# Hybrid encoder on one core: VectorE takes GpSimd's arithmetic in the mixers, and gates, branches and C keys are woven in a new order

## The chip, the core and the metric

The kernel runs on one core of a Trainium2 chip, with its engines TensorE (PE), VectorE (DVE), ScalarE (ACT), GpSimd (POOL) and SyncE (SP, which issues nearly all DMAs here). The metric is the device time of one execution in microseconds. Each engine runs its own list of instructions in order and waits on semaphores for the others.

## The reference

Two layers work on 272 tokens (256 on a grid of 4 rows by 64 columns, and 16 learned meta tokens) of width 1024, in float32:

```python
h = h + 0.5 * swiglu(rms_norm(h, ffn1_norm[l]), ffn1_w_in[l], ffn1_w_out[l])
h = h + hybrid_mixer(rms_norm(h, mix_norm[l]), ...)
h = h + 0.5 * swiglu(rms_norm(h, ffn2_norm[l]), ffn2_w_in[l], ffn2_w_out[l])
```

The mixer projects the normed tokens once into queries, keys and values for three attentions and into three gates, and sums the gated branches:

```python
qa, ka, va, qb, kb, vb, qc, kc, vc, gates = jnp.split(n @ w_in, offsets, axis=-1)
oa = window_sink_attention(rope(qa), rope(ka), va, sink)       # 8 query heads, 2 key heads, |i-j| <= 128
ob = neighbourhood_attention(qb, kb, vb, rpb)                  # 8 heads, 4 x 16 window, learned bias
oc = dense_block_attention(axial_rope(rms_norm(qc)), axial_rope(rms_norm(kc)), vc)
up = einsum('blnc,ncd->blnd', stack([oa, ob, oc]), w_branch)
return sum_n(sigmoid(gates) * up) @ w_out
```

Heads are 64 wide; d_ff is 2816. The last layer's outputs for meta tokens are not needed, so there 256 tokens are queried and 272 are keys.

## The kernel before

Activations lie transposed: features on the 128 partitions, tokens along the free dimension, so a matmul has 272 columns (256 where the meta tokens have dropped out). Float32 accuracy is made from two roundings: a weight block `raw` of 128x1024 is copied by ScalarE into a rounded `hi` (line 250) and the remainder `lo = raw - hi` is computed by VectorE (line 251). `mm` then issues three matmuls per block: hi by the rounded activations (L295), hi by their remainder (L296), lo by the rounded activations (L297). A projection to 256 features from 1024 (`plain(w, 0, 8, c0)`, two weight units of 128x1024) is 8 x 2 x 3 = 48 matmuls; a branch (`branch_rows`, one unit) is 24. The accumulators `acc` have two buffers, the score banks `s` three, weights `hi` and `lo` four each.

Inside the mixer every third plain unit's subtract goes to GpSimd (`lo_engine`), and units that are rearranged while they are split (`turned`, `pairs`: lines 236 to 248) give half of their subtracts to GpSimd. GpSimd also does one step of each rotary embedding (L787 for A, L835 for C) and one of the sums of gated branches (L909).

The mixer's order in the program is: the values, keys and queries of B (values and keys scaled by the row's norm at L762 and L766, queries at L773); then three attentions, each a generator that yields after the scores of one half of the heads for one block of 128 queries. Between two yields `weave` calls the next item of a list: during B the keys of A, the keys of C, both halves of A's queries; during A both halves of C's queries and then gates with branches of B; during C those of A; then those of C and `w_out`.

One step of an attention has the score matmuls (L518 for A and C, L684 for B) into banks `s`; VectorE's pass over each bank (L419 with mask, sink and minimum, or for C L424 and L425); ScalarE's exponential with its sum (L421, L426); VectorE's reciprocal (L438) and normalisation (L439, and L531 for the meta columns). One step later TensorE transposes the normalised `p` (L541; L696 in B), and after every second step multiplies by the values (L449, L454), and the result is split into `oh` and `ol` (L310, L311).

`gated(b, mp)` is a gate projection (48 matmuls), its scaling (L901), a tanh on ScalarE (L902), the branch (24 matmuls) and the product (L907). `c_keys` is a projection, its scaling (L842, L843), a square on ScalarE, matmuls that sum it over a head (L846), a reciprocal square root (`rsqrt`: square root on ScalarE, reciprocal L316 and one Newton step on VectorE), the rotary step and `stack_k` (L477, L479).

The order on each engine isn't that of the program alone: the framework's scheduler places instructions by their dependences and its own estimates of what they take, so matmuls of a woven projection stand between the scores and transposes of the attention. DMAs of weights go through SyncE's queue.

Of the kernel before, what the change touches and what calls it, by code (L numbers as in the profile page):

```python
# [17 lines left out]
D = 1024  # L18
# [74 lines left out]
def encoder_kernel(ctx: ExitStack, tc: tile.TileContext, x, meta_tokens, ffn1_norm, ffn1_w_in, ffn1_w_out,  # L93
# [57 lines left out]

    h = big.tile([128, 8, T], F32, name="h")
# [54 lines left out]
    sink = const.tile([128, DEPTH, 8], F32, name="sink")  # L207


    in_mixer = [False]  # L210
    unit_no = [0]

    def lo_engine():

        unit_no[0] += 1
        return POOL if in_mixer[0] and unit_no[0] % 3 == 0 else DVE

    def unit(nk, loads, pairs=False, turned=False):
# [9 lines left out]
        if turned:  # L228
# [3 lines left out]
            for g in range(2):  # L232
                for b in range(2):
# [3 lines left out]
                    (DVE if g else POOL).tensor_tensor(l_, r_, h_.bitcast(F32), op=ALU.subtract)  # L237
            if not pairs:
                hv, rv, lv = (t[:, :n].rearrange("p (k c) -> p k c", k=nk)[:, :, 128:] for t in (hi, raw, lo))
                ACT.copy(hv, rv)  # L240
                lo_engine().tensor_tensor(lv, rv, hv.bitcast(F32), op=ALU.subtract)
        elif pairs:
# [3 lines left out]
            for g in range(2):  # L246
                ACT.copy(hv[:, :, :, g], rv[:, :, g])
                (DVE if g else POOL).tensor_tensor(lv[:, :, :, g], rv[:, :, g], hv[:, :, :, g].bitcast(F32), op=ALU.subtract)
        else:
            ACT.copy(hi[:, :n], raw[:, :n])  # L250
            lo_engine().tensor_tensor(lo[:, :n], raw[:, :n], hi[:, :n].bitcast(F32), op=ALU.subtract)  # L251
# [61 lines left out]
    def rsqrt(dst, v, tmp):  # L313
# [5 lines left out]
        DVE.tensor_scalar(tmp, tmp, -0.5, 1.5, op0=ALU.mult, op1=ALU.add)  # L319
# [94 lines left out]
    def scores(p, i, s, den, mx, add, start, scale):  # L414
# [89 lines left out]
    def grouped(br, q, kk, vt, oh, ol, masks, mask_m, sinks, sink_m, rq, meta_queries):  # L504
# [3 lines left out]
        if rq is None:  # L508
            nsink = small()
            DVE.tensor_scalar(nsink, sinks, -1.0, None, op0=ALU.mult)  # L510

        def products(qi, half, pm):
            p, mx, den = wide(), small(), small()
            for i in range(4):
# [5 lines left out]
                if rq is None:  # L520
                    scores(p, i, s, den, mx, masks[qi], nsink[:, 4 * g + t:4 * g + t + 1], None)
# [37 lines left out]
        def meta_products():  # L559
# [3 lines left out]
            for g in range(2):  # L563
                for half in range(2):
                    DVE.tensor_copy(qm[:, g, g, half * 32:half * 32 + 32].rearrange("p (t j) -> p t j", t=2),
                                    q[half][:, g, :, GRID:])
# [8 lines left out]
            if rq is None:  # L575
                nsm = small()[:, :1]
                DVE.tensor_scalar(nsm, sink_m, -1.0, None, op0=ALU.mult)
# [455 lines left out]
```

## Time and profile before

| | us |
|---|---|
| median of 3 runs (1338.96 to 1340.93) | 1339.12 |
| the profiled execution | 1339.12 |
| its span | 1337.3 |
| TensorE busy, 10683 matmuls | 1308.9 |
| VectorE busy | 903.7 |
| ScalarE busy | 671.4 |
| GpSimd busy | 170.4 |

The granted clock of TensorE is 0.996 over the span. In rows of groups stand the line, engine, operation, output and inputs, shapes and count, then busy time and the mean of one in nanoseconds, then the engine's idle time before the group and what ended it. Rows in order of time begin with start and length in microseconds from the span's start. "PE busy" counts a matmul to its modelled end; in a steady stream the next one starts before that.

### The profile page before, as it was taken

The page shows a single profiled execution, that of the slowest core. Times are in us where ns is not written, and L with a number is a line of the kernel's source. Part 1 is how long each engine was busy: PE and PEld are TensorE (multiplying, and loading weights), DVE is VectorE, ACT ScalarE, POOL GpSimd, SP SyncE. Part 2 cuts the span into 40 slices and gives each one's busy share as a digit, 9 for nine tenths or more (in the row PEclk, how much of TensorE's full clock was granted, in tenths as well). Part 3 has the DMA queues.
Part 4 walks back from the last instruction along what each step waited for, and adds up shares of the span by engine and source line. Part 5 has one row for each costly group of instructions (what it writes and reads, how often), then busy time and mean ns, then how long its engine had stood idle before and what let it go on. Part 6 is the DMA issues. An engine that isn't in the chain of part 4 may idle for free. (4 is left out here: it accounts for less than half of the span.)

```text
span 1337.3 us, 26009 instructions
## 1 busy us (share of the span) xinstructions
PE 1308.9 (98%) x10683; PEld 1285.8 (96%) x10683; DVE 903.7 (68%) x1352; ACT 671.4 (50%) x1009; POOL 170.4 (13%) x115
## 2 busy tenths in 40 slices
PE   9999999988999999999999999999989999999997
PEld 8999999978999999999999999999889999999997
DVE  6655668699664587646676646677897567765663
ACT  6443444476554455434455434454776545543444
POOL 1000001332122220000000000022422233000000
PEclk9999999999999999999999999999999999999998
DMA  7765555532343676555565555555324456666652
GB/s 232 210 186 174 175 177 181 152 98 93 111 142 111 185 192 189 183 174 174 162 185 174 174 177 179 158 181 158 95 96 128 141 174 188 186 187 187 187 172 78
DMA packets 239010, 217.52 MB, mean 163 GB/s; under 512 B 24804, under 2 KB 237980, under 8 KB 238764
## 3 DMA queue, kind: packets, MB, share of 16 engines
q1 hardware_dynamic: 238540, 215.20, 53.1%
q8 instruction: 84, 1.38, 0.4%
q10 hardware_dynamic: 352, 0.66, 0.1%
q14 instruction: 34, 0.28, 0.1%
HBM read 214.78 MB, written 1.05 MB: 161 GB/s over the span
## 5 line engine op out<-in xcount | busy, mean ns | idle before, releaser
L250 ACT CAST hi<-raw 128x1024 fp32r<-128x1024 f32 (+1 forms) x386 | 398.6, 1033 | 551.6 <-PE acc L296 374.9
L296 PE MATMUL acc<-xl,hi 128*128 128x272 f32 (+1 forms) x2160 | 620.8, 287 | 0.0
L297 PE MATMUL acc<-xh,lo 128*128 128x272 f32 (+1 forms) x2160 | 619.2, 287 | 0.6 <-DVE lo L251 0.6
L295 PE MATMUL acc<-xh,hi 128*128 128x272 f32 (+1 forms) x2160 | 618.2, 286 | 0.6 <-DVE qk L766 0.6
L251 DVE TENSOR_TENSOR lo<-raw,hi 128x1024 fp32r<-128x1024 f32 (+1 forms) x349 | 424.1, 1216 | 215.3 <-ACT hi L250 213.0
L295 PEld LDWEIGHTS acc<-xh,hi 128*128 128x128 f32 x2160 | 408.1, 189 | 3.1 <-issue 2.7
L297 PEld LDWEIGHTS acc<-xh,lo 128*128 128x128 f32 x2160 | 406.8, 188 | 1.5 <-DVE lo L251 0.8
L296 PEld LDWEIGHTS acc<-xl,hi 128*128 128x128 f32 x2160 | 406.5, 188 | 1.1 <-issue 0.7
L296 PE MATMUL acc<-hl,hi 128*128 128x272 f32 (+1 forms) x704 | 201.9, 287 | 0.0
L297 PE MATMUL acc<-hh,lo 128*128 128x272 f32 (+1 forms) x704 | 201.1, 286 | 0.0
L295 PE MATMUL acc<-hh,hi 128*128 128x272 f32 (+1 forms) x704 | 200.4, 285 | 0.0
L295 PEld LDWEIGHTS acc<-hh,hi 128*128 128x128 f32 x704 | 132.7, 189 | 0.1
L297 PEld LDWEIGHTS acc<-hh,lo 128*128 128x128 f32 x704 | 132.3, 188 | 0.0
L296 PEld LDWEIGHTS acc<-hl,hi 128*128 128x128 f32 x704 | 132.2, 188 | 0.0
L251 POOL TENSOR_TENSOR lo<-raw,hi 128x1024 fp32r<-128x1024 f32 x37 | 91.6, 2475 | 229.2 <-ACT hi L250 217.4
L349 POOL TENSOR_TENSOR ss<-ss,scr 128x544 f32<-128x544 f32 (+1 forms) x12 | 17.4, 1448 | 602.2 <-ACT scr L346 602.1
L295 PE MATMUL acc<-oh,hi 128*128 128x272 f32 (+1 forms) x192 | 54.7, 285 | 0.0
L296 PE MATMUL acc<-ol,hi 128*128 128x272 f32 (+1 forms) x192 | 54.7, 285 | 0.0
L297 PE MATMUL acc<-oh,lo 128*128 128x272 f32 (+1 forms) x192 | 54.5, 284 | 0.0
L401 DVE TENSOR_TENSOR scr<-acc,scr 128x544 f32<-128x544 f32 (+1 forms) x40 | 28.6, 716 | 31.0 <-PE acc L297 30.9
L304 DVE SCALAR_TENSOR_TENSOR h<-acc,h 128x544 f32<-128x544 f32 (+1 forms) x40 | 28.5, 714 | 28.4 <-PE acc L297 28.3
L398 DVE TENSOR_TENSOR scr<-acc,rstd 128x544 f32<-128x544 f32 (+1 forms) x40 | 28.6, 716 | 26.2 <-PE acc L297 26.2
(257 smaller groups left out, 1367.1 us busy)
## 6 DMA issues: line engine op xcount, KB each, us to landing
raw<-in_ffn_w_in_dram SPq DMA_DIRECT2D x176, 512.0 KB, 3.6
raw<-in_ffn_w_out_dram SPq DMA_DIRECT2D x80, 512.0 KB, 3.4
raw<-in_w_in_dram SPq DMA_DIRECT2D x80, 512.0 KB, 3.8
raw<-in_w_in_dram SPq DMA_DIRECT2D x32, 256.0 KB, 3.2
raw<-in_w_branch_dram SPq DMA_DIRECT2D x32, 256.0 KB, 4.0
raw<-in_w_out_dram SPq DMA_DIRECT2D x16, 512.0 KB, 3.8
raw<-in_ffn_w_out_dram SPq DMA_DIRECT2D x16, 256.0 KB, 2.7
raw<-in_w_branch_dram SPq DMA_DIRECT2D x8, 512.0 KB, 3.4
```

The lines of the kernel that those rows point to most:

```text
L250: ACT.copy(hi[:, :n], raw[:, :n])
L251: lo_engine().tensor_tensor(lo[:, :n], raw[:, :n], hi[:, :n].bitcast(F32), op=ALU.subtract)
L295: PE.matmul(o, a, rh, start=k == 0, stop=False)
L296: PE.matmul(o, a, rl, start=False, stop=False)
L297: PE.matmul(o, b, rh, start=False, stop=k == len(rows) - 1)
L304: DVE.scalar_tensor_tensor(hv, a[:, :, :n], 0.5, hv, op0=ALU.mult, op1=ALU.add)
L349: (DVE if j == 3 else POOL).tensor_tensor(ss, ss, dst, op=ALU.add)
L398: DVE.tensor_tensor(g, gate, rb, op=ALU.mult)
L401: DVE.tensor_tensor(g, up, g, op=ALU.mult)
```

## The change

- Inside the mixers VectorE does all of GpSimd's arithmetic: the subtracts of `unit`, the rotary steps and the addition of branch A. GpSimd keeps memsets and, outside the attentions, the sums of squares of a norm (L349).
- The keys of C are computed among B's projections, between B's keys and B's queries.
- A gate and its branch are two functions, and three plans say which pieces follow which yield: in B the keys of A, a half of A's queries, a gate, the other half, another gate; in A branches of B, C's queries and two gates; in C the pairs of branch A and two gates of branch C.
- Small operations: copies of meta columns go from VectorE to ScalarE; the sinks are reordered and negated once; a few scalings by a constant (`tensor_scalar`) become operations that read the constant from a tile `cc`; the factor 0.125 of C's queries is folded into the constant under the root.

```diff
@@ -148,6 +148,10 @@
     POOL.memset(ones, 1.0)
+
+    cc = const.tile([128, 4], F32, name="cc")
+    for i, v in enumerate((1.5, HD * EPS, -1.0)):
+        POOL.memset(cc[:, i:i + 1], v)
...
-    def lo_engine():
-
-        unit_no[0] += 1
-        return POOL if in_mixer[0] and unit_no[0] % 3 == 0 else DVE
+    sinks_tg = const.tile([128, 2, DEPTH * 8], F32, name="sinks_tg")
...
-                    (DVE if g else POOL).tensor_tensor(l_, r_, h_.bitcast(F32), op=ALU.subtract)
+                    DVE.tensor_tensor(l_, r_, h_.bitcast(F32), op=ALU.subtract)
...
-                (DVE if g else POOL).tensor_tensor(lv[:, :, :, g], rv[:, :, g], hv[:, :, :, g].bitcast(F32), op=ALU.subtract)
+                DVE.tensor_tensor(lv[:, :, :, g], rv[:, :, g], hv[:, :, :, g].bitcast(F32), op=ALU.subtract)
...
             ACT.copy(hi[:, :n], raw[:, :n])
-            lo_engine().tensor_tensor(lo[:, :n], raw[:, :n], hi[:, :n].bitcast(F32), op=ALU.subtract)
+            DVE.tensor_tensor(lo[:, :n], raw[:, :n], hi[:, :n].bitcast(F32), op=ALU.subtract)
...
-        DVE.tensor_scalar(tmp, tmp, -0.5, 1.5, op0=ALU.mult, op1=ALU.add)
+        DVE.scalar_tensor_tensor(tmp, tmp, -0.5, cc[:, :1].to_broadcast(list(tmp.shape)), op0=ALU.mult, op1=ALU.add)
...
-            DVE.tensor_scalar(mx[:, i:i + 1], mx[:, i:i + 1], scale, -1.0, op0=ALU.mult, op1=ALU.mult)
+            DVE.scalar_tensor_tensor(mx[:, i:i + 1], mx[:, i:i + 1], scale, cc[:, 2:3], op0=ALU.mult, op1=ALU.mult)
...
-        DVE.tensor_copy(vrep, vt[:, None, GRID:].to_broadcast([128, 8, META]))
+        ACT.copy(vrep, vt[:, None, GRID:].to_broadcast([128, 8, META]))
...
-                e = small()
-                DVE.tensor_copy(e[:, :4].rearrange("p (t g) -> p t g", g=2),
-                                sinks.rearrange("p (g t) -> p t g", g=2)[:, 2 * half:2 * half + 2, :])
-                add_sinks(den, mx, e[:, :4], 4)
+                add_sinks(den, mx, sinks[:, 4 * half:4 * half + 4], 4)
...
-            POOL.tensor_tensor(dst, dst, t, op=ALU.add)
+            DVE.tensor_tensor(dst, dst, t, op=ALU.add)
...
-            POOL.tensor_tensor(dst, u, bc(tb[:, 0, :n], m), op=ALU.mult)
+            DVE.tensor_tensor(dst, u, bc(tb[:, 0, :n], m), op=ALU.mult)
...
-                DVE.tensor_copy(sqm[:, 2 * half:2 * half + 2, :], sq[:, :, GRID:])
+                ACT.copy(sqm[:, 2 * half:2 * half + 2, :], sq[:, :, GRID:])
...
-                DVE.tensor_scalar(rqv[:, :nq], rqv[:, :nq], 1.0 / HD, EPS, op0=ALU.mult, op1=ALU.add)
+
+                DVE.tensor_tensor(rqv[:, :nq], rqv[:, :nq], cc[:, 1:2].to_broadcast([128, nq]), op=ALU.add)
                 rsqrt(rq[:, :nq], rqv[:, :nq], t24[:, :nq])
-                DVE.tensor_scalar(rq[:, :nq], rq[:, :nq], 0.125, None, op0=ALU.mult)
...
+        c_keys()
+        qb = q_tile()
+        for half in range(2):
+            a = proj(plain(w, 0, 8, B_Q + half * 256), n_out)
...
-        def gated(b, mp):
+        gates = {}
+
+        def gate(b, mp):
+            g = gates[b, mp] = sb.tile([128, 2, T], F32, name=nm("gate"), tag="gate", bufs=2)[:, :, :n_out]
+            a = proj(plain(w, 0, 8, GATES + b * D + mp * 256), n_out)
+            DVE.tensor_tensor(g, a[:, :, :n_out], rb[:, :, :n_out], op=ALU.mult)
+            ACT.activation(g, g, AF.Tanh, scale=0.5)
+
+        def branch(b, mp):
...
-                POOL.tensor_tensor(tt, tt, g, op=ALU.add)
+                DVE.tensor_tensor(tt, tt, g, op=ALU.add)
...
-        def weave(attention, others):
-
+        def weave(attention, plan):
+
+            plan = list(plan)
             for _ in attention:
-                if others:
-                    others.pop(0)()
-
-        others = [a_keys, c_keys, lambda: a_queries(0), lambda: a_queries(1)]
-        weave(neighbourhood(biases, qb, kb, vb, oh, ol, not last), others)
-        others += [lambda: c_queries(0), lambda: c_queries(1)]
-        others += [lambda mp=mp: gated(1, mp) for mp in range(4)]
-        weave(mix_a(), others)
-        others += [lambda mp=mp: gated(0, mp) for mp in range(4)]
-        weave(mix_c(), others)
-        others += [lambda mp=mp: gated(2, mp) for mp in range(4)]
-        for work in others:
-            work()
+                for work, *which in (plan.pop(0) if plan else ()):
+                    work(*which)
+            for pieces in plan:
+                for work, *which in pieces:
+                    work(*which)
+
+
+        weave(neighbourhood(biases, qb, kb, vb, oh, ol, not last),
+              [[(a_keys,)], [(a_queries, 0)], [(gate, 1, 0)], [(a_queries, 1)], [(gate, 1, 1)]])
+        weave(mix_a(),
+              [[(branch, 1, 0), (c_queries, 0)], [(branch, 1, 1), (gate, 1, 2)], [(c_queries, 1)],
+               [(branch, 1, 2), (gate, 1, 3)], [(branch, 1, 3)]])
+        weave(mix_c(), [[(gate, 0, mp), (branch, 0, mp)] for mp in range(4)] + [[(gate, 2, 0), (gate, 2, 1)]])
+        for mp in range(4):
+            if mp > 1:
+                gate(2, mp)
+            branch(2, mp)
```

More of the change, by code (lines that the diff above doesn't have):

```diff
@@ L240, in unit @@
                 ACT.copy(hv, rv)
-                lo_engine().tensor_tensor(lv, rv, hv.bitcast(F32), op=ALU.subtract)
+                DVE.tensor_tensor(lv, rv, hv.bitcast(F32), op=ALU.subtract)
         elif pairs:
@@ L508, in grouped @@
         if rq is None:
-            nsink = small()
-            DVE.tensor_scalar(nsink, sinks, -1.0, None, op0=ALU.mult)
+            sinks, nsink = sinks
         def products(qi, half, pm):
@@ L520, in products @@
                 if rq is None:
[L521 removed]
+                    scores(p, i, s, den, mx, masks[qi], nsink[:, 2 * t + g:2 * t + g + 1], None)
                 else:
@@ L564, in meta_products @@
                 for half in range(2):
-                    DVE.tensor_copy(qm[:, g, g, half * 32:half * 32 + 32].rearrange("p (t j) -> p t j", t=2),
-                                    q[half][:, g, :, GRID:])
+                    ACT.copy(qm[:, g, g, half * 32:half * 32 + 32].rearrange("p (t j) -> p t j", t=2),
+                             q[half][:, g, :, GRID:])
             s = bank("s", 3)[:, :T]
@@ L576, in meta_products @@
                 nsm = small()[:, :1]
-                DVE.tensor_scalar(nsm, sink_m, -1.0, None, op0=ALU.mult)
+                DVE.tensor_tensor(nsm, sink_m, cc[:, 2:3], op=ALU.mult)
             scores(p, 0, s, den, mx, mask_m, nsm, None if rq is None else rq[:, 16:17])
@@ L646, in neighbourhood @@
             vrep = sb.tile([128, 4, 8, META], F32, name=nm("vrb"), tag="pts", bufs=PTS)
-            DVE.tensor_copy(vrep, vb[:, :, 0, None, 160:].to_broadcast([128, 4, 8, META]))
+            ACT.copy(vrep, vb[:, :, 0, None, 160:].to_broadcast([128, 4, 8, META]))
             pt = bank("s", 3)
@@ L729, in mixer @@
             late_dma(sink, sink_a.partition_broadcast(128))
+            for i in range(DEPTH):
+                DVE.tensor_copy(sinks_tg[:, 0, 8 * i:8 * i + 8].rearrange("p (t g) -> p t g", g=2),
+                                sink[:, i, :].rearrange("p (g t) -> p t g", g=2))
+            DVE.tensor_scalar(sinks_tg[:, 1], sinks_tg[:, 0], -1.0, None, op0=ALU.mult)
         vb = qk(4, 2, KB)
@@ L767, in mixer @@
                                       bc(r[:, GRID:], 2), op=ALU.mult)
-        for half in range(2):
-            a = proj(plain(w, 0, 8, B_Q + half * 256), n_out)
-            for qi in range(2):
-                o = qb[:, 2 * half:2 * half + 2, qi * 128:(qi + 1) * 128]
-                back = bass.AP(tensor=o.tensor, offset=o.offset + 127, ap=[list(o.ap[0]), list(o.ap[1]), [-1, 128]])
-                DVE.tensor_tensor(back, a[:, :, qi * 128:(qi + 1) * 128], bc(r[:, qi * 128:(qi + 1) * 128], 2),
-                                  op=ALU.mult)
-            if not last:
-                DVE.tensor_tensor(qb[:, 2 * half:2 * half + 2, GRID:], a[:, :, GRID:T], bc(r[:, GRID:], 2),
-                                  op=ALU.mult)
         tab = None
@@ L816, in mix_a @@
                 DVE.tensor_reduce(sink_m, t8, axis=AX, op=ALU.add)
-            return grouped(0, qa, ka[0], va, oh, ol, (C("mask_a0"), C("mask_a1")), C("mask_am"), sink[:, l, :],
+            return grouped(0, qa, ka[0], va, oh, ol, (C("mask_a0"), C("mask_a1")), C("mask_am"),
+                           [sinks_tg[:, i, 8 * l:8 * l + 8] for i in range(2)],
                            sink_m, None, not last)
@@ L898, in gated @@
                 halves.extend([qk(4, T, dt=F32R) for _ in range(2)] for _ in range(2))
-            g = sb.tile([128, 2, T], F32, name=nm("gate"), tag="gate", bufs=2)[:, :, :n_out]
-            a = proj(plain(w, 0, 8, GATES + b * D + mp * 256), n_out)
-            DVE.tensor_tensor(g, a[:, :, :n_out], rb[:, :, :n_out], op=ALU.mult)
-            ACT.activation(g, g, AF.Tanh, scale=0.5)
+            g = gates.pop((b, mp))
             a = acc_tile()
```

13 lines of the change are left out of this document (8 added, 5 removed).

## The prediction

> **What bounds the kernel now.** The page comes first: its span and its busy line.
>
> ```profile
> span 1337.3 us, 26009 instructions
> PE 1308.9 (98%) x10683; PEld 1285.8 (96%) x10683; DVE 903.7 (68%) x1352; ACT 671.4 (50%) x1009; POOL 170.4 (13%) x115
> ```
>
> TensorE is busy for 98% of the span, so nothing that only makes another engine faster can pay more than TensorE's own idle time. The next view is the table by stretches, cut at the stages of the two mixers (first layer, then second): projections of B, attention B with its woven work, attention A, attention C, and the gates and w_out behind them. Columns: width of the stretch, then busy time and count on each engine.
>
> ```profile
> core 0: us, PE busy (x) PEld busy (x) DVE busy (x) ACT busy (x) POOL busy (x), PEclk, DMA share, GB/s
> 211.28:248.21 36.93, 36.93 (x295) 36.77 (x294) 28.05 (x55) 16.55 (x25) 10.78 (x8) 1.00 0.63 190
> 248.21:297.35 49.14, 44.40 (x372) 39.07 (x369) 41.30 (x111) 34.36 (x88) 16.99 (x17) 1.00 0.30 87
> 297.35:359.90 62.55, 58.17 (x488) 55.59 (x488) 53.05 (x123) 37.92 (x77) 15.38 (x8) 1.00 0.34 105
> 359.90:424.26 64.36, 63.09 (x531) 60.83 (x530) 40.40 (x80) 34.24 (x66) 16.01 (x8) 1.00 0.43 123
> 424.26:487.10 62.84, 62.22 (x498) 61.51 (x496) 39.97 (x45) 29.32 (x36) 19.02 (x11) 1.00 0.63 182
> 891.82:922.15 30.33, 29.69 (x243) 29.46 (x242) 23.03 (x45) 12.88 (x21) 8.30 (x7) 1.00 0.58 171
> 922.15:967.01 44.86, 42.04 (x332) 37.65 (x331) 37.68 (x94) 32.56 (x84) 16.10 (x15) 0.96 0.36 108
> 967.01:1016.98 49.97, 46.49 (x421) 44.49 (x419) 41.78 (x104) 34.52 (x73) 14.79 (x8) 1.00 0.33 107
> 1016.98:1066.08 49.10, 49.10 (x439) 47.78 (x437) 32.39 (x69) 29.10 (x58) 11.87 (x6) 1.00 0.44 129
> ```
>
> Width less PE busy is the idle time: 0 + 4.74 + 4.38 + 1.27 + 0.62 in the first layer, 0.64 + 2.82 + 3.48 + 0 in the second, 17.95 us together, 15.4 of them in attentions B and A. A little more is lost unseen: a matmul of the projections is booked at 0.29 us, but the next one starts after 0.125 us (36.93 us for 295), so each stop hides some 0.16 us. With stops of about 0.75 us that is 24 stops and 4 us. I put what TensorE loses in the mixers at **22 us**; that is the most this change can win.
>
> Who is late? The waits of TensorE in the first layer's attentions B and A name VectorE:
>
> ```profile
> PEld s L541 <- DVE sm L419: 4.0, 2, 2.2
> PEld s L684 <- DVE sm L419: 2.7, 2, 2.1
> ```
>
> L541 transposes the normalised probabilities p; L684 needs a free score bank, which VectorE empties at L419. Why VectorE is late shows in the order of time, VectorE's rows first, then GpSimd's:
>
> ```profile
> 307.06 3.44 DVE L439 TENSOR_TENSOR p<-p,sm 128x1024 f32<-128x1024 f32 x1
> 310.42 1.37 DVE L531 TENSOR_TENSOR pm<-p,sm 128x64 f32<-128x64 f32 x1
> ...
> 320.92 1.22 DVE L439 TENSOR_TENSOR p<-p,sm 128x1024 f32<-128x1024 f32 x1
> 322.06 0.22 DVE L531 TENSOR_TENSOR pm<-p,sm 128x64 f32<-128x64 f32 x1
> ...
> 324.06 2.34 DVE L883 TENSOR_SCALAR rqv<-rqv 128x17 f32<-128x17 f32 x1
> ...
> 307.04 2.37 POOL L251 TENSOR_TENSOR lo<-raw,hi 128x1024 fp32r<-128x1024 f32 x1 [8.73 <-ACT hi L250]
> 309.37 2.34 POOL L835 TENSOR_TENSOR scr<-scr,tab 128x544 f32<-128x544 f32 x1
> 323.59 2.78 POOL L251 TENSOR_TENSOR lo<-raw,hi 128x1024 fp32r<-128x1024 f32 x1 [3.47 <-ACT hi L250]
> ```
>
> The same two operations take 1.22 and 0.22 us at 320.92, with GpSimd idle, and 3.44 and 1.37 us at 307.06. The first ends 1.1 us after GpSimd's subtract (307.04 + 2.37 = 309.41), its own length, and the second just after GpSimd's multiply (311.71). A scaling of 17 elements takes 2.34 us and ends with GpSimd's subtract at 326.4. VectorE is held while GpSimd computes, and the two largest stops of TensorE in attention A stand behind these two places.
>
> **The change part by part.** *GpSimd's arithmetic goes to VectorE.* The groups kept apart by shape give both sides:
>
> ```profile
> L251 DVE TENSOR_TENSOR lo<-raw,hi 128x1024 fp32r<-128x1024 f32 x333 | 413.1, 1241 | 198.6 <-ACT hi L250 196.2 <-issue 2.0
> L251 POOL TENSOR_TENSOR lo<-raw,hi 128x1024 fp32r<-128x1024 f32 x37 | 91.6, 2475 | 229.2 <-ACT hi L250 217.4 <-DVE tot L907 11.8
> L251 DVE TENSOR_TENSOR lo<-raw,hi 128x512 fp32r<-128x512 f32 x16 | 11.1, 692 | 16.8 <-ACT hi L250 16.8
> L248 DVE TENSOR_TENSOR lo<-raw,hi 128x512 fp32r<-128x512 f32 x8 | 9.7, 1227 | 0.0
> L439 DVE TENSOR_TENSOR p<-p,sm 128x1024 f32<-128x1024 f32 x16 | 24.4, 1523 | 0.4
> L531 DVE TENSOR_TENSOR pm<-p,sm 128x64 f32<-128x64 f32 x16 | 9.0, 563 | 0.0
> L311 DVE TENSOR_TENSOR qk<-tot,qk 128x512 fp32r<-128x512 f32 x4 | 8.5, 2129 | 2.7 <-ACT qk L310 2.7
> L349 POOL TENSOR_TENSOR ss<-ss,scr 128x544 f32<-128x544 f32 (+1 forms) x12 | 17.4, 1448 | 602.2 <-ACT scr L346 602.1
> ```
>
> A subtract that costs GpSimd 2.475 us costs VectorE 1.241, half. Of GpSimd's 170.4 us only the sums of squares (17.4) and some 6 us of memsets and final sums stay, so 147 us move and cost VectorE about 74. In return the stretched operations shrink: 16 x (1.523 - 1.22) = 4.8, 16 x (0.563 - 0.22) = 5.5, 8 x (1.227 - 0.692) = 4.3, 4 x (2.129 - 0.692) = 5.7, and 2.1 for the 17 elements: 22 us, some 5 in each B and A stretch. VectorE thus gains about 50 us of work; whether TensorE waits for it is a question of place.
>
> [...]
>
> GpSimd's list in the first layer from the loading of the C queries to attention A (L248, L251 split weights, L787 and L835 are rotary steps), before:
>
> ```order
> L248 TENSOR_TENSOR lo_3573<-raw_3571,hi_3572 128x8x64
> L787 TENSOR_TENSOR scr_3326<-scr_3326,scr_3327 128x544
> L251 TENSOR_TENSOR lo_3745<-raw_3743,hi_3744 128x1024
> L835 TENSOR_TENSOR scr_3502<-scr_3492,tab_3504 128x544
> L835 TENSOR_TENSOR scr_3642<-scr_3629,tab_3504 128x544
> L251 TENSOR_TENSOR lo_3888<-raw_3886,hi_3887 128x1024
> ```
>
> and GpSimd's whole list from the constants to the next layer's start, now:
>
> ```order
> L154 MEMSET cc 128x1 x3
> L555 MEMSET qm_4133 128x256
> L617 MEMSET qk_2310 128x8x16
> L617 MEMSET qk_2329 128x8x16
> L346 ISA
> L346 TENSOR_TENSOR ss_119<-ss_119,scr_184 128x544
> L346 TENSOR_TENSOR ss_119<-ss_119,scr_189 128x544
> L346 TENSOR_TENSOR ss_199<-ss_199,scr_2124 128x544
> L346 TENSOR_TENSOR ss_199<-ss_199,scr_2211 128x544
> L555 MEMSET qm_4846 128x256
> ```
>
> Nothing on GpSimd can hold VectorE inside a mixer any more.
>
> *The C keys move ahead of the B queries.* They take 48 matmuls (6 us of TensorE), two weight splits (2.5 us) and on VectorE some 15 operations of 272 columns at 0.434 and a reciprocal of 1.852, 8.4 us: together 11. Today's projections leave room for that, as the wait in the first row shows:
>
> ```profile
> 248.40 0.75 DVE L773 TENSOR_TENSOR qk<-acc,rstd 128x256 f32<-128x256 f32 x2 [3.91 <-PE acc L297]
> L316 DVE RECIPROCAL scr<-scr 128x272 f32<-128x272 f32 x2 | 3.7, 1852 | 1.9 <-ACT scr L315 1.9
> L479 DVE TENSOR_TENSOR qk<-scr,qk 64x272 fp32r<-64x272 f32 x16 | 6.9, 434 | 1.6 <-ACT qk L477 1.4
> ```
>
> VectorE has 36.93 - 28.05 = 8.9 us idle there. With the move it has 28.05 + 11 + half of GpSimd's 10.78 less 2 of stretches = 42.4 us to do, in 36.93 + 6 = 42.9 of TensorE; the second layer 23.03 + 11 + 4.2 - 2 = 36.2, in 29.69 + 5.6 = 35.3. This is the **tightest place** of the new kernel, and a chain through it is serial (scale, square on ScalarE, matmul, square root, reciprocal). VectorE's list where the projections end, before (L773 scales the B queries, L237 and L241 split the A keys' weights, L137 empties banks with B's turned values):
>
> ```order
> L773 TENSOR_TENSOR qk_2343<-acc_2702,rstd_2410 128x2x128 x2
> L776 TENSOR_TENSOR qk_2343<-acc_2702,rstd_2410 128x2x16
> L251 TENSOR_TENSOR lo_2989<-raw_2987,hi_2988 128x1024
> L137 COPY vk_2772<-s_2767 88x512
> L137 COPY vk_2786<-s_2781 88x512
> ```
>
> and now (L476 stacks the C keys, L883 scales the B queries):
>
> ```order
> L476 TENSOR_TENSOR qk_2725<-scr_2715,qk_2725 64x272 x4
> L886 TENSOR_TENSOR qk_2734<-acc_2747,rstd_2417 128x2x16
> L234 TENSOR_TENSOR lo_2972<-raw_2970,hi_2971 128x4x2x16
> L238 TENSOR_TENSOR lo_2972<-raw_2970,hi_2971 128x4x128
> L883 TENSOR_TENSOR qk_2734<-acc_2811,rstd_2417 128x2x128 x2
> L886 TENSOR_TENSOR qk_2734<-acc_2811,rstd_2417 128x2x16
> L137 COPY vk_2875<-s_2870 88x512
> L137 COPY vk_2889<-s_2884 88x512
> ```
>
> The tail of the C keys now stands ahead of the last B queries and of the banks that TensorE needs next. I cost this at a new stop of 2 us in each layer; the bounds are 0 (the 42.4 fit into 42.9) and 4 (all of the chain's waits fall on TensorE).
>
> *Gates apart from branches.* In B the C keys' 11 us of VectorE are replaced by two gates, each two splits and a scaling, 2 x (2.48 + 0.72) = 6.4 (0.72 is an estimate for 544 columns from 0.692 for 512). VectorE in B: 41.30 - 5 + 8.5 - 11 + 6.4 = 40.2 against TensorE's 44.40 + 5.3 = 49.7 (one projection more, less the keys' small matmuls); second layer 37.68 - 5 + 8 - 11 + 6.4 = 36.1 against 46.9. A: 53.05 - 5 + 7.7 - 1.2 (a gate fewer, a branch more) - 2 (small operations) = 52.5 against 58.17 - 3.0 = 55.2; second layer, with two branches more (2 x 1.96, and 5.6 of TensorE), 41.78 - 5 + 7.4 + 3.9 - 2 = 46.1 against 52.1. C: 40.40 + 8 of GpSimd's + 1.2 - 1 = 48.6 against 66, and with two gates more 32.39 + 5.9 + 6.4 = 44.7 against 60.3. So B gets a cover of 10 us, A of 3 to 6, and C has plenty.
>
> *Small operations.* Copies to ScalarE, the sinks reordered once, and the multiply by 0.125 folded away: about 2 us less of VectorE in each A, counted above. ScalarE is busy 34.36 of 49.14 in B, so the few short copies it takes cost nothing; were it full, they would cost their own length, by estimate 1 us in each layer. The C keys' square root no longer stands among exponentials, which spares ScalarE two table loads per layer at 1.28 us:
>
> ```profile
> L315 ACT ACT_TABLE_LOAD x11 | 14.1, 1283 | 0.2
> L421 ACT ACT_TABLE_LOAD x5 | 6.4, 1283 | 0.1
> ```
>
> That is off TensorE's path except where the next exponential is late; I count nothing.
>
> *The sum.* TensorE's work is the same, so the time is today's less the change in lost time. Left over I expect: the start of B 2 + 2, B 1.5 + 1, A 2.5 + 1.5 (its steps with C queries still ask more of VectorE than of TensorE), C and the gates 1.5, and 1 unseen: 13 us of today's 22. The gain is 9. The profiled execution took 1339.12 us, which is also the median, with a span of 1337.3; 1339.1 - 9 = **1330 us**. With 0 to 4 at each start of B and the other leftovers between a third and twice, its own range is 1325 to 1336.
>
> **The rivals.** *Nearly every stop goes.* If the stretches were the whole cause, only C's 1.3 us and some 2 remain: 1339.1 - 22 + 3 = 1320. For it: both large stops in A stand behind a stretch. Against: the 42.4 of 42.9.
>
> *VectorE becomes the bound (slower).* Stretches in B and A show VectorE at 84, 85, 84 and 84% (41.30 of 49.14, and so on). If it can do no better under such chains, the projections need 42.4 / 0.84 = 50.5 and 43.1, A 62.5 and 54.9: 7.6 + 7.8 + 7.3 + 2.8 = 25.5 us lost, 28.5 with C and the unseen, 6.5 more than now: 1346. Below a share of about 87% the change loses. Against it stand these rows, where VectorE has a backlog and is 99% busy:
>
> ```profile
> 224.00:236.00 12.00, 12.00 (x98) 12.00 (x98) 11.86 (x28) 4.21 (x4) 2.39 (x1) 1.00 0.40 126
> 300.00:330.00 30.00, 25.62 (x200) 24.16 (x199) 29.73 (x74) 20.73 (x47) 8.82 (x4) 1.00 0.28 89
> ```
>
> *It doesn't do what it says.* The stops could come from the in-order list of TensorE, which meets a transpose or a bank before the softmax chain behind it is through, stretch or none. Then moving steps about exchanges stops for others: 1337 to 1339.
>
> **How the numbers follow.** Chances: the forecast 0.54, nearly all stops gone 0.22, no effect 0.12, VectorE the bound 0.12. A measurement here tells about 0.2% (2.7 us) from no change. Below 1336.4 lie the first two and a little of the third: faster 0.78; the rest of the third 0.11; slower 0.11. The range is 1320 to 1338: it takes in most of the second case and the upper end of the forecast, and leaves out the fourth.
>
> **What would show it.** Right: GpSimd's busy time falls to about 23 us and VectorE's rises to about 950; L439 shows 1.22 us throughout and L531 0.22; table loads fall from 22 to 18; the idle of TensorE in B and A falls from 15.4 to some 6; a stop of 1 to 3 us appears between the last B query and the first score of B. Wrong: TensorE's stops behind L541's and L696's counterparts stay though no operation is stretched (the third rival), or VectorE is full through projections and A with TensorE waiting more than 22 us (the second).

## The result and the profile after

The changed kernel takes **1319.38 us** (median of 4 runs, 1319.24 to 1320.88) against 1339.07 us before on the same chip: a ratio of 0.985, interval 0.984 to 0.9865, 19.7 us less. The forecast was 1330 (1320 to 1338): right in sign, with less than half of the gain, and the median lies 0.6 us below the range. The second case, "Nearly every stop goes" at 1320 with a chance of 0.22, gave the time that came.

The profiled execution took 1320.88 us. Its span and busy line, and the chain of work that ended last by engine, from the page of the kernel after:

```profile
span 1318.7 us, 25909 instructions
PE 1304.1 (99%) x10683; PEld 1284.6 (97%) x10683; DVE 923.6 (70%) x1418; ACT 667.3 (51%) x1020; POOL 22.1 (2%) x28
...
PE 95%; DVE 2%; ACT 1%; issue 0%; DMA 0%; ACTq 0%; DVEq 0%
```

GpSimd is down to 22.1 us (some 23 were expected), VectorE up to 923.6 (950 were expected), and TensorE alone makes 95% of the chain. The table by stretches, kernel after, cut again at projections, attention B, A, C, and the gates with `w_out`, first layer and then second:

```profile
core 0: us, PE busy (x) PEld busy (x) DVE busy (x) ACT busy (x) POOL busy (x), PEclk, DMA share, GB/s
209.05:256.10 47.05, 46.37 (x365) 45.62 (x363) 41.72 (x85) 24.39 (x41) 1.47 (x1) 1.00 0.54 170
256.10:304.27 48.17, 48.17 (x416) 44.25 (x415) 40.35 (x111) 32.55 (x85) 0.00 (x0) 1.00 0.40 121
304.27:358.01 53.74, 53.74 (x468) 52.65 (x466) 46.07 (x114) 36.09 (x83) 0.32 (x1) 1.00 0.42 122
358.01:424.10 66.09, 66.09 (x554) 63.72 (x553) 47.19 (x91) 35.61 (x67) 0.41 (x2) 1.00 0.44 125
424.10:477.61 53.51, 51.48 (x400) 50.78 (x399) 37.65 (x45) 24.35 (x31) 2.84 (x2) 0.97 0.57 169
882.33:919.29 36.96, 36.35 (x295) 35.98 (x294) 31.68 (x68) 18.01 (x33) 0.00 (x0) 1.00 0.51 157
919.29:964.33 45.04, 44.88 (x386) 40.89 (x385) 38.57 (x100) 31.68 (x80) 0.00 (x0) 1.00 0.43 129
964.33:1014.92 50.59, 50.50 (x456) 49.44 (x455) 44.27 (x105) 34.32 (x73) 0.00 (x0) 1.00 0.42 126
1014.92:1071.00 56.08, 56.08 (x497) 54.47 (x496) 42.35 (x81) 32.57 (x62) 0.00 (x0) 1.00 0.45 133
```

In attentions B and A of both layers width less TensorE's busy time is 0 + 0 + 0.16 + 0.09 = 0.25 us, where it was 15.4. The largest idle time left is the 2.03 us in the fifth row. Counted another way, in the mixers, the starts of matmuls that come more than 0.34 us after the one before add up to 21.8 us above the steady 0.125 in the kernel before, and to 5.1 in the kernel after: 16.7 of the span's 18.6 us. Below, "counted stops" are such sums, and a single stop is given whole, from the start of one matmul to the start of the next.

The groups of VectorE kept apart by shape (count, busy us and mean ns of one, then idle time) answer to the stretched rows before; L436 is the normalisation, L524 that of the meta columns, L308 the remainder `ol` and its like, L245 and L234 the splits of rearranged units:

```profile
L248 DVE TENSOR_TENSOR lo<-raw,hi 128x1024 fp32r<-128x1024 f32 x370 | 453.1, 1225 | 204.4 <-ACT hi L247 203.7
L436 DVE TENSOR_TENSOR p<-p,sm 128x1024 f32<-128x1024 f32 x16 | 19.6, 1224 | 0.5
L245 DVE TENSOR_TENSOR lo<-raw,hi 128x512 fp32r<-128x512 f32 x16 | 10.8, 683 | 1.2 <-ACT hi L244 1.2
L234 DVE TENSOR_TENSOR lo<-raw,hi 128x256 fp32r<-128x256 f32 x32 | 11.7, 413 | 0.0
L524 DVE TENSOR_TENSOR pm<-p,sm 128x64 f32<-128x64 f32 x16 | 3.5, 218 | 0.0
L308 DVE TENSOR_TENSOR qk<-tot,qk 128x512 fp32r<-128x512 f32 x4 | 2.7, 684 | 0.0
```

None of them is stretched any more: 1523 ns became 1224, 563 became 218, 1227 became 683, 2129 became 684.

### The profile page after: what moved, and what is told of

The parts are those of the page before. It is cut to its first block, busy times and chain, and to the rows that moved or that the text cites. A ratio compares the mean times of both kernels' runs of the same rounds, so it can differ in the third digit from the quotient of the medians.

```text
span 1318.7 us, 25909 instructions
## 1 busy us (share of the span) xinstructions
PE 1304.1 (99%) x10683; PEld 1284.6 (97%) x10683; DVE 923.6 (70%) x1418; ACT 667.3 (51%) x1020; POOL 22.1 (2%) x28
## 4 chain that ended last, share of the span: by engine, by line
PE 95%; DVE 2%; ACT 1%; issue 0%; DMA 0%; ACTq 0%; DVEq 0%
PE acc L293 29%; PE acc L292 29%; PE acc L294 29%; PE pv L451 2%; PE s L514 1%; PE s L534 1%; DVE lo L248 1%; PE s L677 1%; PE pv L446 1%; PE s L689 1%; PE s L351 0%; DVE qk L757 0%; DMA qk<-in_meta_tokens_dram 0%; ACT hi L247 0%; PE acc L851 0%
## 5 line engine op out<-in xcount | busy, mean ns | idle before, releaser
L248 DVE TENSOR_TENSOR lo<-raw,hi 128x1024 fp32r<-128x1024 f32 (+1 forms) x386 | 464.1, 1203 | 221.1 <-ACT hi L247 220.5
L292 PEld LDWEIGHTS acc<-oh,hi 128*128 128x128 f32 x192 | 36.8, 192 | 0.5 <-ACT oh L307 0.4
L293 PEld LDWEIGHTS acc<-ol,hi 128*128 128x128 f32 x192 | 36.8, 192 | 0.4 <-issue 0.3
```

The costliest lines, as they stand in the source:

```text
L248: DVE.tensor_tensor(lo[:, :n], raw[:, :n], hi[:, :n].bitcast(F32), op=ALU.subtract)
L292: PE.matmul(o, a, rh, start=k == 0, stop=False)
L293: PE.matmul(o, a, rl, start=False, stop=False)
```

## The experiments

Two theories stood at first. **S**: TensorE's stops come from VectorE being held by GpSimd, so moving the arithmetic makes the gain. **O**: they come from the order of steps, so the new order makes it. The first four runs take the change apart.

### The arithmetic alone

The kernel before, with all of GpSimd's arithmetic in the mixers on VectorE and nothing else:

```diff
-        return POOL if in_mixer[0] and unit_no[0] % 3 == 0 else DVE
+        return DVE
-            POOL.tensor_tensor(dst, dst, t, op=ALU.add)
+            DVE.tensor_tensor(dst, dst, t, op=ALU.add)
```

and the same for the halves of the rearranged units, C's rotary step and the addition of branch A.

> The kernel before, with only GpSimd's arithmetic inside the mixers given to VectorE; order of steps and small operations as before. Theory S (the stops of TensorE come from VectorE being held while GpSimd computes): most of the 19.7 us come with this alone, 1322 to 1328, no operation of VectorE stretched; some stops stay in B, where VectorE then has about 45 us of work in 44 of TensorE. Rival O (the order of steps made the gain, the moved arithmetic by itself is a load): VectorE has 50 us more to do in the same places, 1336 to 1345.

It took 1329.98 us, ratio 0.9929 (0.9914 to 0.9944): 9.4 us, half of the gain, between the two theories. From its page and its waits:

```profile
PE 1310.9 (99%) x10683; PEld 1288.0 (97%) x10683; DVE 925.8 (70%) x1442; ACT 671.9 (51%) x1009; POOL 21.9 (2%) x25
```

```profile
PEld s L541 <- DVE sm L419: 3.1, 2, 2.7
```

This run sizes the stretches. VectorE's busy time can't do it, since records of neighbours overlap (the 1352 operations before add up to 959.7 us and keep it busy for 903.7). Compared group by group, the length of each operation before against the mean of its shape here, the stretches come to 41 us, not 22. The counted stops fall from 21.8 to 9.5 us. The largest that is left is where the old order computes C queries and scores of A together: TensorE stands from 304.43 to 307.25, 2.81 us. VectorE's rows in order of time there are all at full speed; TensorE's row stands last:

```profile
303.98 0.17 DVE L867 COPY rqv<-acc 128x8 f32<-128x8 f32 x1 [0.75 <-PE acc L865]
304.07 1.22 DVE L439 TENSOR_TENSOR p<-p,sm 128x1024 f32<-128x1024 f32 x1
...
305.42 0.72 DVE L835 TENSOR_TENSOR scr<-scr,tab 128x544 f32<-128x544 f32 x1
306.05 0.72 DVE L836 TENSOR_TENSOR scr<-scr,tab 128x544 f32<-128x544 f32 x1
306.69 0.50 DVE L419 CUSTOM_DVE_ANT_0 p<-s,cst,sm 128x272 f32<-128x272 f32 x1
...
307.25 1.96 PE L541 MATMUL s<-cst,p 128*128 128x128 f32 x7 [2.40 <-DVE sm L419]
```

VectorE stands 0.75 us for TensorE at L867, with the normalisation behind it in line. The normalised p is ready at 305.29, but the transposes of L541 also need a free score bank, and the pass of L419 that empties one stands behind two rotary steps of C. They start at 307.25, just behind that pass: with no operation stretched, this stop comes from the order.

### GpSimd's arithmetic restored under the new order

The changed kernel with GpSimd's arithmetic restored by the old rule (the reverse of the edit above):

> The changed kernel with GpSimd's arithmetic back (every third subtract, half of the rearranged ones, one rotary step, the addition of branch A); new order of steps and small operations kept. S: the stretched operations return (L439's counterpart near 1.5 us on the mean) and with them most of the stops, 1330 to 1337. O: the order keeps the gain, 1320 to 1325.

It took 1349.5 us, ratio 1.0072 (1.0057 to 1.0087). The order and the small operations together cost 10 us where GpSimd computes, and pay 10.6 (1329.98 - 1319.38) where it doesn't. Neither theory has room for that sign; the last two runs below settle it.

### The C keys back among B's steps

```diff
-        c_keys()
         qb = q_tile()
-              [[(a_keys,)], [(a_queries, 0)], [(gate, 1, 0)], [(a_queries, 1)], [(gate, 1, 1)]])
+              [[(a_keys,)], [(c_keys,)], [(a_queries, 0)], [(gate, 1, 0)], [(a_queries, 1)], [(gate, 1, 1)]])
```

> The changed kernel with the C keys back among B's woven steps (between A's keys and the first half of A's queries), nothing else. S: B has room (40 us of VectorE against 48 of TensorE, plus 11 against 6), 1319 to 1323, and the table loads rise from 18 to 22. O, with the C keys' place as its main part: the stops of 2 us behind the keys' chain return in both layers, 1324 to 1330.

1323.59 us, ratio 0.9879 (0.9864 to 0.9894): the keys' new place is worth about 4 us by the medians (the interval just touches the change's), where the prediction had charged it with 4.

### Gates glued to their branches again

```diff
-              [[(branch, 1, 0), (c_queries, 0)], [(branch, 1, 1), (gate, 1, 2)], [(c_queries, 1)],
-               [(branch, 1, 2), (gate, 1, 3)], [(branch, 1, 3)]])
+              [[(c_queries, 0)], [(c_queries, 1)]] + [[(gate, 1, mp), (branch, 1, mp)] for mp in range(4)])
```

with the gates taken out of B's plan and C's in the same way.

> The changed kernel with each gate glued to its branch again (B: keys of A and both halves of its queries; A: both halves of C's queries, then gate and branch together; C as before), the C keys still among the projections. S: 1319 to 1323. O, with the spread of gates as its main part: attention A is short of TensorE work beside C's queries again, 1325 to 1330.

1326.94 us, ratio 0.9906 (0.989 to 0.9923): the spread of the gates is worth 7.6 us by the medians. The stops return in attention A; from its waits and, in order of time, VectorE's rows:

```profile
PEld pv L446 <- DVE pmt L545: 3.7, 4, 2.5
```

```profile
318.76 0.72 DVE L896 TENSOR_TENSOR gate<-acc,rstd 128x544 f32<-128x544 f32 x1
319.85 0.27 DVE L313 RECIPROCAL rq<-rq 128x17 f32<-128x17 f32 x1 [0.36 <-ACT rq L312]
...
320.38 1.47 DVE L466 TENSOR_TENSOR qk<-scr,qk 64x544 fp32r<-64x544 f32 x2 [0.25 <-ACT qk L465]
...
321.97 0.28 DVE L545 COPY pmt<-s 128x128 f32<-128x128 f32 x1
```

The copy of L545, 0.28 us long, is what TensorE needs (a stop of 2.54 us at 319.77), and it stands behind C's root and the stacking of C's queries. The counted stops rise by 3.4 us and the span of the profiled execution by 5.6, so this place explains a part of the 7.6.

### Which part of GpSimd's work does the harm

Two runs give back to GpSimd, in the changed kernel, the weight subtracts alone and the rest alone (rotary steps and the addition of branch A). **H** is the theory that what hurts is a GpSimd step inside a serial chain, not the holding of VectorE.

> The changed kernel with only the weight subtracts given back to GpSimd, by the old rule (every third plain unit in the mixers, half of the rearranged ones); the rotary steps and the addition of branch A stay on VectorE. Theory S (VectorE's operations stand still while GpSimd reads SBUF): these subtracts are about 115 of the 144 us of GpSimd's work that costs the changed order 30 us, so they bring most of it back: 1338 to 1346. Theory H (what hurts is a GpSimd step inside a serial chain, which others wait for: the rotary steps ahead of the stacking of keys and queries): the subtracts have slack, 1320 to 1327.

> The changed kernel with only the rotary steps and the addition of branch A given back to GpSimd; all weight subtracts stay on VectorE. These are about 27 us of GpSimd's work. Theory S: about a fifth of the 30 us, 1322 to 1328. Theory H: most of the 30 us, 1338 to 1347.

The subtracts: 1341.66 us, ratio 1.0014 (1.0004 to 1.0023), 22 us worse than the changed kernel; the rest: 1329.29 us, 0.9919 (0.9903 to 0.9936), 10 us worse. GpSimd is busy for 143.6 and 48.3 us in them, 121 and 26 us more than after the change: the loss per microsecond of GpSimd's work is 0.18 and 0.38. Both parts hurt, the rest more per microsecond than S foresaw, the subtracts more than H allows.

The traces say why the rest costs so much, and most of it isn't H. Of the 9.2 us by which its counted stops exceed the changed kernel's, 5.9 are eight stops in attention C, each beside or just behind one of GpSimd's eight additions of branch A. Six of them stand behind a held product of C, the one-column operation of the last two runs below. GpSimd's row and VectorE's at the first:

```profile
375.14 1.37 POOL L912 TENSOR_TENSOR tot<-tot,gate 128x544 f32<-128x544 f32 x1 [20.23 <-DVE gate L910]
375.67 0.98 DVE L422 SCALAR_TENSOR_TENSOR sm<-sm,rq,cc 128x1 f32<-128x1 f32 x2
```

The first of the two products takes 0.86 us instead of 0.21 and ends with the addition, and TensorE's next scores start 0.83 us after the matmul before them. In the run with the subtracts two stops of some 2.4 us in C stand behind the same product, held for 2.32 us. So both losses contain a price that the kernel before doesn't pay, since its product has another form. Six stops in attention B of the run with the rest, 3.9 us, come after rotary steps; whether they are holds or H wasn't separated.

### Work on GpSimd that nobody waits for

The next three leave the lists of TensorE, VectorE and ScalarE exactly those of the changed kernel, and add redundant work on GpSimd in the mixers (36 places by the trace), 8 short subtracts:

```diff
+                if unit_no[0] % 3 == 0:
+                    POOL.tensor_copy(noise[:, :1], hi[:, :1].bitcast(F32))
+                    for _ in range(8):
+                        POOL.tensor_tensor(noise[:, :92], ones[:, :92], ones[:, :92], op=ALU.subtract)
```

> The changed kernel with work on GpSimd that no other engine waits for: behind every third plain unit's ScalarE copy in the mixers (37 places) GpSimd copies one column of it and then does 8 subtracts of 128x92 from SBUF to SBUF, about 2.4 us together. Its results are not used. VectorE's and TensorE's lists are those of the changed kernel. Theory S, if reading alone holds VectorE: VectorE's operations with two SBUF inputs are stretched again where they meet it (the normalisation back from 1.22 us towards 1.5 in the mean), and the time goes to 1330 to 1345. Theory H: nothing waits for it, 1319 to 1323.

or 13 memsets in their place:

> The same as the run before it, with 13 memsets of 128x92 in place of the 8 subtracts: GpSimd is as busy but reads nothing from SBUF. Theory S, reading alone: 1319 to 1322, no operation of VectorE stretched. If any access of GpSimd holds VectorE, the same as with the subtracts: 1330 to 1345. Theory H: 1319 to 1323.

or one long subtract into the dead raw block:

```diff
+                if unit_no[0] % 3 == 0:
+                    POOL.tensor_tensor(raw[:, :n], raw[:, :n], hi[:, :n].bitcast(F32), op=ALU.subtract)
```

> The changed kernel with one long redundant operation on GpSimd in 37 places of the mixers: behind every third plain unit's subtract on VectorE GpSimd repeats it over 128x1024 into the raw block, which nobody reads any more. VectorE's, TensorE's and ScalarE's lists are those of the changed kernel; a raw block comes free some 2.4 us later. Theory L (VectorE stands still for one whole operation of GpSimd, so a long one hurts where eight short ones did not): the normalisation and other operations with two SBUF inputs are stretched again by up to 2.4 us each where they meet it, and the time goes to 1328 to 1340. Theory H (what costs is that the work that others wait for is slower on GpSimd and stands elsewhere): nothing waits for it, 1319 to 1323.

They took 1322.04 us (0.987, 0.9855 to 0.9885), 1320.71 (0.9859, 0.9845 to 0.9874) and 1336.92 (0.9988, 0.998 to 0.9997); the first two intervals overlap that of the changed kernel. With its list unchanged VectorE is busy for 928.7, 923.0 and 965.8 us, against 923.6. Groups by shape of the normalisation on VectorE and of the added work on GpSimd, first with the short subtracts:

```profile
L445 DVE TENSOR_TENSOR p<-p,sm 128x1024 f32<-128x1024 f32 x16 | 19.8, 1235 | 0.5
L257 POOL TENSOR_TENSOR noise<-ones 128x92 f32<-128x92 f32 x288 | 149.2, 518 | 22.5
```

and with the long one, with two rows in order of time:

```profile
L442 DVE TENSOR_TENSOR p<-p,sm 128x1024 f32<-128x1024 f32 x16 | 24.5, 1534 | 0.5
L254 POOL TENSOR_TENSOR raw<-raw,hi 128x1024 f32<-128x1024 f32 x36 | 90.4, 2510 | 402.3 <-DVE lo L250 338.8 <-ACT p L424 26.3 <-DVE sm L441 18.4
```

```profile
276.12 2.46 DVE L236 TENSOR_TENSOR lo<-raw,hi 128x256 fp32r<-128x256 f32 x1
...
275.92 2.38 POOL L254 TENSOR_TENSOR raw<-raw,hi 128x1024 f32<-128x1024 f32 x1 [29.57 <-DVE lo L250]
```

This tells them apart. 149 us of short reads cost 2.7 us by the medians; 90 us of long reads, whose result nobody wants, cost 17.5. A subtract of 256 columns, 413 ns in the mean after the change, takes 2.46 beside the long one and ends 0.28 after it (278.58 against 278.30). In this row VectorE is held to the end of one GpSimd instruction. Its busy time grows by 42 us with the long subtracts and by 5 with the short, which take 8 x 518 ns = 4.1 us in each place, where 2.4 were expected. That a hold of 2.4 us empties what TensorE has ahead of it, while one of some 0.5 doesn't, is the author's estimate from the two times; no row shows a single hold beside a short subtract, and the normalisation grows there only from 1224 to 1235 ns. The 13 memsets, 175 ns each, keep GpSimd busy for 82.0 us in all, not as long as the short subtracts, and the normalisation keeps its length in that run; a long memset wasn't tried:

```profile
L445 DVE TENSOR_TENSOR p<-p,sm 128x1024 f32<-128x1024 f32 x16 | 19.6, 1224 | 0.5
```

What the long subtracts' run doesn't separate is the raw block that comes free later, which can delay a load; no wait of TensorE's in the mixers is put down to a load, but it wasn't tried apart.

### The order without the new form, and the new form without the order

Left was the sign of the second run. In it one operation of C stood out. The change writes the product that makes the exponential's bias (one column per score) as a `scalar_tensor_tensor` with a constant tile; before, it is a `tensor_scalar` with an immediate. Both also take the factor `rq`, one number per partition, from a tile. From the groups of the kernel before, and of the new order under GpSimd's arithmetic:

```profile
L425 DVE TENSOR_SCALAR sm<-sm,rq 128x1 f32<-128x1 f32 x33 | 6.2, 208 | 0.4
```

```profile
L430 DVE SCALAR_TENSOR_TENSOR sm<-sm,rq,cc 128x1 f32<-128x1 f32 x33 | 17.4, 547 | 0.4
```

One run takes the second experiment with the small operations as before, so that the order is all that is new; the other takes the kernel before with this one line:

```diff
-            DVE.tensor_scalar(mx[:, i:i + 1], mx[:, i:i + 1], scale, -1.0, op0=ALU.mult, op1=ALU.mult)
+            DVE.scalar_tensor_tensor(mx[:, i:i + 1], mx[:, i:i + 1], scale, cc[:, 2:3], op0=ALU.mult, op1=ALU.mult)
```

> The kernel before with the new order alone: GpSimd keeps its arithmetic and the small operations keep their old form, among them the one-element product of C (L425 before), a scaling with an immediate that was never stretched in the profile before (208 ns in the mean), while its new form, which reads a second tile, took 547 ns in the mean beside GpSimd's arithmetic. Theory F (the new form, held by GpSimd, made the new order with GpSimd's arithmetic 10 us slower than the kernel before): 1337 to 1343. Theory O2 (the order itself is bad with GpSimd in it, since other steps now meet its subtracts): 1347 to 1351.

> The kernel before with one edit: the one-element product of C reads its constant from a tile, as after the change. Theory F: it is stretched where it meets GpSimd (towards 350 to 550 ns in the mean) and attention C gets stops, 1342 to 1349. Theory O2: 1338 to 1341.

The order alone: 1339.19 us, ratio 0.9997 (0.9986 to 1.0007), no change. The one line: **1347.59 us**, ratio 1.0058 (1.0046 to 1.007), slower by 8.5 us. In order of time, the kernel before in attention C of the second layer, VectorE and then GpSimd:

```profile
1038.66 0.33 DVE L425 TENSOR_SCALAR sm<-sm,rq 128x1 f32<-128x1 f32 x2
...
1039.37 0.21 DVE L425 TENSOR_SCALAR sm<-sm,rq 128x1 f32<-128x1 f32 x1
...
1038.40 2.38 POOL L251 TENSOR_TENSOR lo<-raw,hi 128x1024 fp32r<-128x1024 f32 x1 [8.08 <-ACT hi L250]
```

and with the one line changed:

```profile
1041.29 2.24 DVE L427 SCALAR_TENSOR_TENSOR sm<-sm,rq,cc 128x1 f32<-128x1 f32 x2
...
1041.03 2.37 POOL L253 TENSOR_TENSOR lo<-raw,hi 128x1024 fp32r<-128x1024 f32 x1 [9.68 <-ACT hi L252]
```

In the middle of GpSimd's subtract two of the old form pass in 0.33 us together and a third in 0.21, and two of the new form take 2.24, to just behind the subtract's end at 1043.40; scores, banks and TensorE wait behind it (a stop of 2.03 us at 1042.13). The two forms differ in the instruction and in the second tile that the new one reads; which of the two lets it be held wasn't tried.

### The small operations

The changed kernel with every small operation as before:

> The changed kernel with the small operations as before: copies of meta columns on VectorE, the sinks reordered in each step, scalings by constants and the multiply by 0.125. If they are worth nothing, as the prediction counted: 1318 to 1321. If VectorE's few microseconds decide stops in attention A: 1321 to 1325.

1321.06 us, ratio 0.986 (0.9847 to 0.9874), against 0.9853 (0.984 to 0.9865) for the change: not told apart. Without GpSimd's arithmetic they are worth nothing that can be measured, one way or the other. This run is also the arithmetic and the order without the rest: from 1329.98 to 1321.06 the order gives 8.9 us.

### What is left

Stops over 0.45 us in the mixers of the changed kernel are four: 0.89 and 0.90 us ahead of the third projection of each mixer, whose accumulator is still waiting for the norm's root (B's values are scaled from it), and 1.81 and 0.52 at 424.2. The largest has these rows of ScalarE and TensorE:

```profile
424.10 1.04 ACT L247 CAST hi<-raw 128x1024 fp32r<-128x1024 f32 x1 [1.95 <-PE acc L293]
425.05 0.65 ACT L897 ACTIVATE gate<-gate 128x544 f32<-128x544 f32 x1
425.61 0.35 ACT L135 COPY pts<-s 128x256 f32<-128x256 f32 x1
...
426.02 0.45 PE L605 MATMUL pv<-pts,v 128*64 128x64 f32 x4 [1.54 <-ACT pts L135]
```

A copy of 0.35 us waits behind a weight's rounding and a tanh. Two runs remove these:

```diff
+                    if dst is vb:
+                        a1 = scr()
+                        ACT.copy(a1, a[:, :, :T])
+                        a = a1
```

> The changed kernel in which ScalarE first copies the two accumulators of B's values to SBUF, so that TensorE gets the buffer back without waiting for the row's norm: the stops of 0.89 and 0.90 us ahead of the third projection of each mixer go, 1317 to 1319. If the copy delays ScalarE's weight rounding instead, 1319 to 1321.

```diff
-        evac(pts[:, :256], pt[:, :256])
-        evac(pts[:META, 256:384], pt[:META, 256:384])
+        DVE.tensor_copy(pts[:, :256], pt[:, :256])
+        DVE.tensor_copy(pts[:META, 256:384], pt[:META, 256:384])
```

> The run before it, and the two copies of C's turned meta probabilities both on VectorE instead of one on ScalarE, where it stands behind a weight's rounding: the stop of 1.81 us at 424.2 goes too, 1315 to 1318. If VectorE's list holds them as long: 1317 to 1319.

The first: 1319.38 us, ratio 0.9848 (0.9834 to 0.9861). Both stops ahead of the third projections are gone from its trace, and the median is that of the change. The profiled execution of the change is the slowest of its four, so profile against profile this run is 1.6 us shorter and median against median not at all; what took the stops' place in the other executions wasn't found. Both edits: 1317.98 us, 0.9837 (0.9824 to 0.985), the stop at 424.2 down from 1.81 to 1.09. Its median is the lowest of all, 1.4 us below the change, but the intervals overlap.

Holds are left too, outside the attentions: ten operations of the norms (L336, `xl<-h,gcol,xh`) take 1.51 to 1.61 us beside GpSimd's sums of squares (L346), and the other thirty about 0.5. No run takes these sums off GpSimd. Three of them, at 209.19, 467.84 and 473.90, lie in the mixers' stretches of the table, so "Nothing on GpSimd can hold VectorE inside a mixer any more" came true for the attentions alone. There the longest left on GpSimd is a memset of 0.32 us at 350.99, and the subtract on VectorE that it meets, from 350.06 on, takes its usual 1.22 us.

## Why the prediction was right and wrong

**The bound and the ceiling** were right. TensorE sets the time, what it loses in the mixers is all that could be won, and the 22 us put on that hold: the counted stops were 21.8 us. They fell to 5.1, and the time by 19.7, 3 us more than they did; where those 3 lie wasn't found.

**The sum failed, at "Left over I expect ... 13 us".** Term by term, in TensorE's idle time by stretches:

| term | left over, predicted | measured |
|---|---|---|
| start of B, both layers | 2 + 2 | nothing; stops of 0.35 and 0.36 in the second |
| attention B | 1.5 + 1 | 0 + 0.16 |
| attention A | 2.5 + 1.5 | 0 + 0.09 |
| C and gates | 1.5 | 2.03 |
| projections of B | none | 0.68 + 0.61 |
| unseen | 1 | 1.5 (5.1 counted, 3.57 idle) |

What the sum lacked is the order, worth 8.9 us once GpSimd is silent; the sum charged it with 4 us at the start of B and left 6.5 us of stops in B and A. That 1330 is also what the arithmetic alone gave (1329.98) is chance: the stops left there stand in other places than those of the sum.

**"GpSimd's arithmetic goes to VectorE".** The mechanism was right: held operations fell to full speed (the normalisation from 1523 to 1224 ns), and long subtracts on GpSimd that nobody waits for raised the normalisation to 1534 ns again and the time by 17.5 us. The size was off: the groups that the prediction listed gave 22 us of stretches, and in the run with the arithmetic alone they did shrink by 22.6, but over all operations it is 41. The rest is spread over many that meet GpSimd once or twice, which a list of the worst groups doesn't hold. A mean over a group hides them too: 333 subtracts at 1241 instead of 1225 ns are 5.3 us.

**"Gates apart from branches".** A was put at 52.5 us of VectorE against 55.2 of TensorE in the first layer, 95%; measured are 46.07 of 53.74, 86%. Half of that miss is stretches: 5 us were counted, and group by group they came to 8.2 in that stretch of the kernel before (5.9 in B, and 5.4 and 3.3 in B and A of the second layer). The moved work was put at 7.7, half of GpSimd's time, and its four subtracts and two rotary steps cost VectorE 6.3 (4 x 1.225 + 2 x 0.72). The 2.5 us left over in A were priced for a stretch that is nearly full, and it isn't. In B 40.2 of 49.7 was predicted and 40.35 of 48.17 came, with no stop where 1.5 was allowed. The runs show what the spread does: with gates glued to their branches again the copy that TensorE needs in A stands behind C's root and the stacking of C's queries, and 7.6 us come back by the medians.

**"The C keys move ahead of the B queries", the tightest place.** The demand was right in the first layer (42.4 predicted, 41.72 measured) and too high in the second (36.2, and 31.68 measured), but the stop of 2 us per layer didn't come, and the move paid about 4 us instead of costing 4. Rows of VectorE and then TensorE in the kernel after, in order of time:

```profile
245.69 0.43 DVE L835 TENSOR_SCALAR scr<-acc 128x272 f32<-128x272 f32 x1
...
246.62 1.85 DVE L313 RECIPROCAL scr<-scr 128x272 f32<-128x272 f32 x1
...
256.69 0.74 DVE L883 TENSOR_TENSOR qk<-acc,rstd 128x256 f32<-128x256 f32 x2
...
257.45 1.37 DVE L137 COPY vk<-s 88x512 f32<-88x512 f32 x2
...
256.10 2.00 PE L634 MATMUL s<-cst,qk 128*88 128x128 f32 x16
...
258.77 0.38 PE L652 MATMUL s<-qk,qk 64*16 64x16 f32 x12
```

The reciprocal starts without waiting: the chain through ScalarE, matmul and root is covered by weight splits and the rotary step. And the last queries are scaled at 257.43 (256.69 + 0.74), 1.3 us after the projections' end, while TensorE transposes B's values (16 from 256.10 on), which need neither C keys nor B queries; the first matmul that reads a query starts at 258.77. That cover was not counted. The stop does exist where GpSimd computes: under the same order with GpSimd's arithmetic TensorE has stops of 1.56, 0.94 and 2.60 us at this place, and the order is worth nothing as a whole.

**"Small operations".** Nothing was predicted and nothing is measurable, and table loads fell from 22 to 18 as said. But the reason given was only cover on ScalarE. That a scaling became an operation which reads a constant tile besides was passed over; this one line cost 8.5 us in the kernel before, where GpSimd computes, while after the change, with GpSimd silent in the attentions, the product takes 211 ns in the mean against 208 before.

**The rivals.** "Nearly every stop goes" gave the time but not the reason: with the stretches gone and the old order, 9.5 us of counted stops remain, so the stretches weren't the whole cause. "VectorE becomes the bound" took VectorE's 84% in the old stretches for a sign of what it can do. After the change it stands at 84% in B (40.35 of 48.17) and 86% in A with TensorE never idle, so the share alone said nothing. "It doesn't do what it says" holds for one half of the change by itself: the order under GpSimd's arithmetic moved stops about and won nothing.

## What to carry to other kernels

A GpSimd subtract of 2.4 us cost a neighbour on VectorE nearly its own length here (3.44 us for a normalisation of 1.22, 2.24 for two one-column products that take 0.33 in the old form), so price it at every operation that it can meet, down to a scaling of one column, and not only at the groups that look slow. The form of a small operation mattered where GpSimd computes: here the one-column `tensor_scalar` passes (0.21 us), and the `scalar_tensor_tensor` with a constant tile stands (2.32 us for one, 8.5 us of the kernel's time). And parts of a change multiply: here an order that was worth nothing became worth 9 us when the holds were gone, so size each part with the others already in place.

## What the runs showed of the hardware

- What VectorE lost didn't go by GpSimd's busy time: 149 us of subtracts at 0.52 us each made VectorE busy for 5 us more and cost 2.7 us by the medians, 90 us at 2.51 each made it busy for 42 us more and cost 17.5. The two runs differ in the length of one instruction and in the tiles that it reads. In the rows shown a held operation ends with the one GpSimd instruction that it met or up to 1.1 us after it.
- The `tensor_scalar` of one column isn't held (0.21 us inside a GpSimd subtract), one of 17 columns is (2.34 us, in the prediction's rows; the one of 16 columns in the second layer of the kernel before takes 0.15), though it reads one tile and the expectations speak of operations with two SBUF inputs. The two differ in width, and in that the first takes a factor from a tile where the second has two immediates; which of these decides wasn't tried.
- The short subtracts on GpSimd were long for their size, 518 ns for 92 columns against 2510 for 1024. Whether VectorE holds them in turn, or this is their fixed cost, wasn't tried.
